# Stores of the projection stage on GpSimd's DMA queue, in one step of a hybrid retention and sliding-window layer

## The chip, the core and the metric

The kernel runs on one core of one Trainium2 chip. The metric is the device time of one execution in microseconds, the median of several runs. A core has TensorE (PE, matmuls), VectorE (DVE), ScalarE (ACT), GpSimd (POOL) and SyncE (SP). Each engine takes its instructions in order. DMA transfers are issued as instructions of an engine's queue, and all queues share the core's 16 DMA engines.

## The reference

One inference step of one layer over 1024 prompt tokens and 64 sample tokens, width 1024, in float32. The part that matters here is the mixer's input projection and the retention that follows it:

```python
rq, rk, rv, rg, sq, sk, sv, ga, gb = in_proj(h, g_attn, w_in)   # rms_norm(x) @ w_in, split
q = rope(rq.reshape(B, S, RET_HEADS, RET_DK), pos)
k = rope(rk.reshape(B, S, RET_HEADS, RET_DK), pos) * (RET_DK ** -0.5)
v = rv.reshape(B, S, RET_HEADS, RET_DV)
...
s = jnp.einsum('bihd,bjhd->bhij', q, k) * intra          # inside a chunk
o = jnp.einsum('bhij,bjhe->bihe', s, v)
o = o + jnp.einsum('bihd,bhde->bihe', q, state) * q_dec[None, :, :, None]
new_state = state * jnp.exp(log_gamma * C)[None, :, None, None] + kv
```

Four retention heads of 256, then a sliding-window attention (SWA) of 16 heads over `sq`, `sk`, `sv` with a relative-position bias, then gates, a mix, cross-attention and a SwiGLU feed-forward.

## The kernel before

All 1088 tokens are worked as two halves of 544 columns (`half(t)`), with the features on the 128 partitions. A projection (`strassen`, line 264) multiplies 1024 x 256 weights with the tokens in seven products of 24 matmuls, each operand split into a high and a low part. A product goes to one of three PSUM buffers (`bank_pair`); `taken` (line 594) adds it to a partial sum and writes it to one of eight stage tiles, which go round (`staged`, line 590).

The changed stage is `project_phase` (line 573). It runs, in program order:

- the values of head 0 (`values`, line 641), with plain products;
- for each head: keys and queries with rotation (`rotated`, line 618; four result tiles and four helper tiles each), the values (heads 1 to 3), one pair of SWA queries (`project` with `queries`, lines 602 and 647), then `retention(h)` (line 741);
- SWA's keys and values (line 687);
- the fourth pair of SWA queries, the gates and the memory's keys and values.

Everything that a projection makes is stored to scratch in DRAM and read back later: `d_qkv` (rotated keys, queries, values), `d_sq` (SWA queries, in rows of 64 numbers, 256 bytes), `d_skv`, `d_ret` (retention's output, line 875), and the states `o_rsp` and `o_rss` (lines 820, 848). `bias_table` (line 550) writes `d_rb`, 1 MB from 16 partitions. `retention` reads `d_qkv` back in blocks of 256 tokens into the buffers `ks`, `vf` and `qs`, one of each. Its first step on PE is to turn `ks` and `vf` (`turned`, L738); the scores (`pss`) come next.

For heads 0 and 1 VectorE does the whole rotation (L630 to L636); from head 2 on GpSimd does its last two steps (L635, L636). GpSimd also multiplies the SWA results by `rstd` (L605).

Both `load` (line 116) and `store` (line 119) issue on SyncE, so a store that waits for its data holds up every load behind it. The order of the instructions on each engine is not the program order: the framework lays it out when the program is built (`schedule_with_timeline_sim=True`), and `issue_after` pins a few places. In the retention of one head, the next head's projections are thus mixed in. [...]

```python
nc = bacc.Bacc("TRN2", target_bir_lowering=False, num_devices=1, dynamic_dma_scratch_size=1024)
```

Of the kernel before, what the change touches and what calls it, by code (L numbers as in the profile page):

```python
# [97 lines left out]
class Ring:  # L98


    def __init__(self, pool):
        self.pool, self.next = pool, 0
# [7 lines left out]
class Kernel:  # L110
    def __init__(self, nc, tc, io, decay):
        self.nc, self.tc, self.io, self.decay = nc, tc, io, decay
        self.later = []
        self.refill = None

    def load(self, out, in_):
        return self.nc.sync.dma_start(out, in_).ins

    def store(self, out, in_):
        self.nc.sync.dma_start(out, in_)  # L120

    def split(self, src, hi, lo):
        self.last_cast = self.nc.scalar.copy(hi, src).ins  # L123
# [449 lines left out]
    def project_phase(self):  # L573
        nc, tc, io = self.nc, self.tc, self.io
        with ExitStack() as ctx:
# [11 lines left out]
            half = lambda t: slice(t * HALF, (t + 1) * HALF)  # L587
            flat = lambda o: o.rearrange("p b c -> p (b c)")

            def staged():  # L590
                count[0] += 1
                return stage[(count[0] - 1) % len(stage)]

            def taken(ps, sb):
                o = staged()
                if sb is None:
                    nc.scalar.copy(o, ps)
                else:
                    nc.vector.tensor_tensor(out=o, in0=ps, in1=sb, op=ALU.add)  # L599
                return flat(o)  # L600

            def project(w, put, act=None, other=None):
                def emit(i, t, ps, sb):
                    o = taken(ps, sb)
                    (nc.vector if act is not None else nc.gpsimd).tensor_tensor(  # L605
                        out=o, in0=o, in1=self.rstd[:, half(t)], op=ALU.mult)
                    if act is not None:
                        nc.scalar.activation(o, o, act)
                    if other is not None:
                        r = op.tile([P, HALF], F32, tag="other", bufs=4, name="other")  # L610
                        self.load(r, other(i)[:, half(t)])
                        nc.gpsimd.tensor_tensor(out=o, in0=o, in1=r, op=ALU.mult)
                    put(i, t, o)
                cast = self.last_cast
                self.strassen(w, self.ops, emit)
                return cast

            def rotated(w, h, j):

                done = {}  # L620

                def emit(i, t, ps, sb):
                    done[i, t] = taken(ps, sb)
                    if (1 - i, t) not in done:
                        return
                    a, b = done[0, t], done[1, t]
                    cos, sin = (rope[:, i, half(t)] for i in range(2))
                    sa, sb = flat(staged()), flat(staged())
                    tt = nc.vector.tensor_tensor
                    tt(out=sa, in0=a, in1=sin, op=ALU.mult)  # L630
                    tt(out=sb, in0=b, in1=sin, op=ALU.mult)
                    tt(out=a, in0=a, in1=cos, op=ALU.mult)
                    tt(out=b, in0=b, in1=cos, op=ALU.mult)
                    tt = tt if h < 2 else nc.gpsimd.tensor_tensor
                    tt(out=a, in0=a, in1=sb, op=ALU.subtract)  # L635
                    tt(out=b, in0=b, in1=sa, op=ALU.add)  # L636
                    self.store(self.d_qkv[j, 2 * h, :, half(t)], a)
                    self.store(self.d_qkv[j, 2 * h + 1, :, half(t)], b)
                self.strassen(w, self.ops, emit)

            def values(w, h, by=self.strassen):
                def emit(i, t, ps, sb):
                    self.stores.append(self.load(self.d_qkv[2, 2 * h + i, :, half(t)], taken(ps, sb)))
                by(w, self.ops, emit)

            pair = lambda w, h: self.load_ops([io[w][2 * h + i] for i in range(2)])
            def queries(p):
                def put(i, t, o):
                    d = self.d_sq[p, :, :, i, :]
                    r = lambda x: x.rearrange("p (c q) -> p c q", q=64)  # L650
                    if t == 0:
                        self.store(d[:, 0:8, :], r(o[:, :512]))
                        self.store(d[:, 8, 0:32], o[:, 512:])
                    else:
                        self.store(d[:, 8, 32:64], o[:, :32])
                        self.store(d[:, 9:17, :], r(o[:, 32:]))
                return put

            self.stores = []
# [4 lines left out]
            stage, count = self.stage_tiles(), [0]  # L664
            with ExitStack() as rctx:
                self.ra = rctx.enter_context(tc.tile_pool(name="ra", bufs=1, reuse_waits="tile"))
                rope = self.ra.tile([P, 2, T], F32, name="rope")
                for t in range(2):
                    self.load(rope[:, :, half(t)], io["c_rope"][:, :, half(t)])
                for h in range(H):  # L670
                    rotated(pair("w_k", h) if h else first, h, 1)
                    if h == 0:
                        self.token_squares()
                    rotated(pair("w_q", h), h, 0)
                    if h == 0:
                        self.token_roots()
                        self.retention_setup()
                    else:
                        values(pair("w_v", h), h)
                    if h:  # L680
                        project(pair("w_sq", h - 1), queries(h - 1))
                    self.retention(h)
                    if h == 0:
                        self.spread_roots()
                    if h == 1:
                        self.later.append(self.bias_table)
                project(self.load_ops((io["w_sk"], io["w_sv"])), lambda i, t, o: self.store(self.d_skv[i, :, half(t)], o))
            self.sums_by = nc.gpsimd
            project(pair("w_sq", 3), queries(3))
            steps = [0, 0, 0, 0, 1, 2, 2, 3, 3, 3, 2, 0]  # L690
            for idx, w, act in ((1, "w_ga", AF.Sigmoid), (0, "w_rg", AF.Silu), (2, "w_gb", AF.Sigmoid)):
                for m in range(0, KT, 2):
                    if (idx, m) == (1, 6):
                        fctx.close()
                        self.sixth = self.left.enter_context(tc.tile_pool(name="sixth", bufs=1, reuse_waits="tile"))
                        self.last_held = self.turns
                        self.sums_pool(ctx)
                        op = ctx.enter_context(tc.tile_pool(name="op", bufs=1, reuse_waits="tile"))
                        mp = ctx.enter_context(tc.tile_pool(name="mp", bufs=1, reuse_waits="tile"))
                        self.dense_psum = lambda: self.norm_psum("pd")  # L700
                        memory = self.memory_phase(mp)
                    store = nc.gpsimd.dma_start if (idx, m) == (2, KT - 2) else nc.scalar.dma_start if idx else self.store
                    put = lambda i, t, o, idx=idx, m=m, store=store: store(self.d_gate[idx][m + i, :, half(t)], o)
                    other = None if idx else lambda i, m=m: self.d_ret[m + i]
                    with tc.issue_after(project(pair(w, m // 2), put, act, other)):
                        for i in range(steps.pop(0)):
                            if (idx, m, i) == (0, 6, 0):
                                with tc.issue_after(self.last_mm):
                                    next(memory)
                            else:  # L710
                                next(memory)
# [1125 lines left out]
```

## Time and profile before

| | |
|---|---|
| median of 3 runs | 2172.38 us (2171.64 to 2174.21) |
| the profiled execution | 2174.93 us, its span 2173.1 us |
| PE busy | 2139.7 us, 98% of the span |
| VectorE, ScalarE, GpSimd busy | 71%, 40%, 26% |
| granted clock, mean | 0.996 of full speed |
| SyncE's queue (q1) | 175058 packets, 278.18 MB |
| GpSimd's queue (q0) | 512 packets, 1.64 MB: eight DMAs, all after 780 us |
| the changed stage | from about 40 to 510 us of the span |

How to read it: a row of a timeline has the start in us, the length in us, the engine, the line, the operation, the tiles written and read, and in brackets the idle time before it and what ended that. SPq is SyncE's DMA queue; the length of an issue there is its time on the queue, not that of the transfer. A row of waits has who waited, for whom, the total in us, the number of times and the longest. A row of DMA issues ends with the count, the size of one and the median time from issue to landing.

### The profile page before, as it was taken

The page shows a single profiled execution, that of the slowest core. Times are in us where ns is not written, and L with a number is a line of the kernel's source. Part 1 is how long each engine was busy: PE and PEld are TensorE (multiplying, and loading weights), DVE is VectorE, ACT ScalarE, POOL GpSimd, SP SyncE. Part 2 cuts the span into 40 slices and gives each one's busy share as a digit, 9 for nine tenths or more (in the row PEclk, how much of TensorE's full clock was granted, in tenths as well). Part 3 has the DMA queues.
Part 4 walks back from the last instruction along what each step waited for, and adds up shares of the span by engine and source line. Part 5 has one row for each costly group of instructions (what it writes and reads, how often), then busy time and mean ns, then how long its engine had stood idle before and what let it go on. Part 6 is the DMA issues. An engine that isn't in the chain of part 4 may idle for free.

```text
span 2173.1 us, 41702 instructions
## 1 busy us (share of the span) xinstructions
PE 2139.7 (98%) x16371; PEld 2088.6 (96%) x16371; DVE 1546.5 (71%) x2870; ACT 876.2 (40%) x1900; POOL 562.2 (26%) x438
## 2 busy tenths in 40 slices
PE   9999999999999999999999999999999999999997
PEld 9999999999999997889999999999999999999997
DVE  8996978776677568656545465768777776777588
ACT  7444434244434347543233343333222222344243
POOL 0001211232253223430000000014565555523531
PEclk9999999999999999999999999999999999999999
DMA  6444453444345476327443111422343333384333
GB/s 225 146 140 118 128 139 110 138 130 153 118 144 171 161 223 224 117 87 228 123 152 103 40 54 54 153 81 91 126 132 106 105 103 114 100 327 144 120 113 114
DMA packets 180373, 290.83 MB, mean 134 GB/s; under 512 B 40178, under 2 KB 109202, under 8 KB 180178
## 3 DMA queue, kind: packets, MB, share of 16 engines
q1 hardware_dynamic: 175058, 278.18, 40.3%
q10 hardware_dynamic: 4608, 8.36, 1.0%
q8 instruction: 129, 2.11, 0.4%
q0 software_dynamic: 512, 1.64, 0.2%
q14 instruction: 66, 0.54, 0.1%
HBM read 196.95 MB, written 91.16 MB: 133 GB/s over the span
## 4 chain that ended last, share of the span: by engine, by line
PE 88%; DVE 5%; DMA 3%; ACT 2%; issue 2%; POOL 0%; SPq 0%; POOLq 0%; DVEq 0%; ACTq 0%
PE pq L225 18%; PE pq L223 18%; PE pq L222 18%; PE pd L156 8%; PE pd L158 7%; PE pd L157 7%; PE pout L1037 1%; PE pss L974 1%; DVE wq L124 1%; DMA hl<-d_op 1%; PE pk L738 1%; PE pp L1013 1%; DMA ld<-d_swa 1%; PE po L158 1%; PE po L157 1%
## 5 line engine op out<-in xcount | busy, mean ns | idle before, releaser
L124 DVE TENSOR_TENSOR wq<-raw,wq 128x512 fp32r<-128x512 f32 (+1 forms) x499 | 437.9, 882 | 134.8 <-ACT wq L123 131.7
L123 ACT CAST wq<-raw 128x512 fp32r<-128x512 f32 (+1 forms) x499 | 301.9, 614 | 539.0 <-PE pq L225 189.2
L223 PE MATMUL pq<-T,wq 128*128 128x272 f32 x1832 | 492.9, 289 | 0.0
L222 PE MATMUL pq<-T,wq 128*128 128x272 f32 x1832 | 491.3, 288 | 0.6 <-ACT wq L123 0.6
L223 PE MATMUL pq<-B,wq 128*128 128x272 f32 x1592 | 428.3, 289 | 2.1 <-DVE B L124 1.9
L222 PE MATMUL pq<-B,wq 128*128 128x272 f32 x1592 | 427.0, 288 | 0.5 <-ACT B L123 0.3
L225 PE MATMUL pq<-T,wq 128*128 128x272 f32 x1832 | 384.0, 290 | 0.9 <-DVE wq L124 0.9
L222 PEld LDWEIGHTS pq<-T,wq 128*128 128x128 f32 x1832 | 345.2, 188 | 1.2 <-issue 0.8
L223 PEld LDWEIGHTS pq<-T,wq 128*128 128x128 f32 x1832 | 344.9, 188 | 0.9 <-issue 0.8
L225 PE MATMUL pq<-B,wq 128*128 128x272 f32 x1592 | 332.2, 289 | 1.1 <-DVE wq L124 1.1
L223 PEld LDWEIGHTS pq<-B,wq 128*128 128x128 f32 x1592 | 299.8, 188 | 3.2 <-DVE B L124 2.7
L222 PEld LDWEIGHTS pq<-B,wq 128*128 128x128 f32 x1592 | 299.5, 188 | 1.0 <-ACT B L123 0.9
L225 PEld LDWEIGHTS pq<-T,wq 128*128 128x128 f32 x1832 | 290.7, 190 | 2.4 <-DVE wq L124 1.1
L200 POOL TENSOR_TENSOR raw<-raw 128x512 f32<-128x512 f32 (+1 forms) x44 | 64.1, 1457 | 832.3 <-DVE rs_r L311 485.6
L225 PEld LDWEIGHTS pq<-B,wq 128*128 128x128 f32 x1592 | 252.4, 190 | 2.5 <-DVE wq L124 1.3
L269 DVE TENSOR_TENSOR u<-pq,u 128x544 f32<-128x544 f32 x177 | 127.2, 719 | 80.9 <-PE pq L225 80.7
L605 POOL TENSOR_TENSOR stage<-stage,rstd 128x544 f32<-128x544 f32 x20 | 31.5, 1582 | 319.8 <-ACT rstd L500 205.6
L599 DVE TENSOR_TENSOR stage<-pq,u 128x544 f32<-128x544 f32 x112 | 80.5, 719 | 33.6 <-PE pq L225 29.1
L156 PE MATMUL pd<-xc,wq 128*128 128x256 f32 (+1 forms) x256 | 74.6, 291 | 0.0
L158 PE MATMUL pd<-xc,wq 128*128 128x256 f32 (+1 forms) x256 | 74.2, 290 | 0.0
L1485 POOL TENSOR_TENSOR stage<-stage,rstd_f 128x544 f32<-128x544 f32 x40 | 63.9, 1608 | 39.1 <-ACT stage L1484 39.1
L157 PE MATMUL pd<-xc,wq 128*128 128x256 f32 (+1 forms) x256 | 73.8, 288 | 0.0
(385 smaller groups left out, 4559.3 us busy)
## 6 DMA issues: line engine op xcount, KB each, us to landing
hl<-d_op SPq DMA_DIRECT2D x85, 272.0 KB, 5.0
d_qkv<-stage SPq DMA_DIRECT2D x44, 272.0 KB, 2.5
d_op<-stage SPq DMA_DIRECT2D x44, 272.0 KB, 2.3
d_op<-ht SPq DMA_DIRECT2D x44, 272.0 KB, 4.0
raw<-w_gate SPq DMA_DIRECT2D x22, 512.0 KB, 3.6
raw<-w_up SPq DMA_DIRECT2D x22, 512.0 KB, 4.9
raw<-w_down SPq DMA_DIRECT2D x16, 512.0 KB, 4.6
d_gate<-stage ACTq DMA_DIRECT2D x28, 272.0 KB, 2.8
```

Source lines behind the costliest of these rows:

```text
L123: self.last_cast = self.nc.scalar.copy(hi, src).ins
L124: return self.nc.vector.tensor_tensor(out=lo, in0=src, in1=hi.bitcast(F32), op=ALU.subtract).ins
L156: mm(ps, wh, xh, start=start, stop=False)
L157: mm(ps, wh, xl, start=False, stop=False)
L158: self.last_mm = mm(ps, wl, xh, start=False, stop=stop).ins
L200: tt(out=a11, in0=a11, in1=a21, op=sub)
L222: mm(ps[:, c, :HC], w[:, 0, ks], x[:, 0, cs], start=start, stop=False)
L223: mm(ps[:, c, :HC], w[:, 0, ks], x[:, 1, cs], start=False, stop=False)
L225: self.last_mm = mm(ps[:, c, :HC], w[:, 1, ks], x[:, 0, c * HC:(c + 1) * HC], start=False, stop=stop).ins
L269: add = lambda out, a, b: nc.vector.tensor_tensor(out=out, in0=a, in1=b, op=ALU.add)
L599: nc.vector.tensor_tensor(out=o, in0=ps, in1=sb, op=ALU.add)
L1485: nc.gpsimd.tensor_tensor(out=g, in0=g, in1=r[t], op=ALU.mult)
```

## The change

A new field `store_by` names the engine that issues stores. It is SyncE at first, GpSimd from the first rotated keys on until SWA's keys and values have been projected, and SyncE again from the fourth pair of SWA queries on. `values` now calls `store` where it called `load` (which also issues on SyncE) for its stores. In `queries`, the store of 8 blocks of 64 tokens becomes two of 4 blocks; the short stores of 32 tokens stay. Loads are untouched.

```diff
@@ -112,12 +112,13 @@
         self.nc, self.tc, self.io, self.decay = nc, tc, io, decay
         self.later = []
         self.refill = None
+        self.store_by = nc.sync
 
     def load(self, out, in_):
         return self.nc.sync.dma_start(out, in_).ins
 
     def store(self, out, in_):
-        self.nc.sync.dma_start(out, in_)
+        return self.store_by.dma_start(out, in_).ins
 
     def split(self, src, hi, lo):
         self.last_cast = self.nc.scalar.copy(hi, src).ins
@@ -640,7 +641,7 @@
 
             def values(w, h, by=self.strassen):
                 def emit(i, t, ps, sb):
-                    self.stores.append(self.load(self.d_qkv[2, 2 * h + i, :, half(t)], taken(ps, sb)))
+                    self.stores.append(self.store(self.d_qkv[2, 2 * h + i, :, half(t)], taken(ps, sb)))
                 by(w, self.ops, emit)
 
             pair = lambda w, h: self.load_ops([io[w][2 * h + i] for i in range(2)])
@@ -649,11 +650,13 @@
                     d = self.d_sq[p, :, :, i, :]
                     r = lambda x: x.rearrange("p (c q) -> p c q", q=64)
                     if t == 0:
-                        self.store(d[:, 0:8, :], r(o[:, :512]))
+                        for q in range(0, 8, 4):
+                            self.store(d[:, q:q + 4, :], r(o[:, q * 64:q * 64 + 256]))
                         self.store(d[:, 8, 0:32], o[:, 512:])
                     else:
                         self.store(d[:, 8, 32:64], o[:, :32])
-                        self.store(d[:, 9:17, :], r(o[:, 32:]))
+                        for q in range(0, 8, 4):
+                            self.store(d[:, 9 + q:13 + q, :], r(o[:, 32 + q * 64:288 + q * 64]))
                 return put
 
             self.stores = []
@@ -664,6 +667,7 @@
             stage, count = self.stage_tiles(), [0]
             with ExitStack() as rctx:
                 self.ra = rctx.enter_context(tc.tile_pool(name="ra", bufs=1, reuse_waits="tile"))
+                self.store_by = nc.gpsimd
                 rope = self.ra.tile([P, 2, T], F32, name="rope")
                 for t in range(2):
                     self.load(rope[:, :, half(t)], io["c_rope"][:, :, half(t)])
@@ -685,7 +689,7 @@
                     if h == 1:
                         self.later.append(self.bias_table)
                 project(self.load_ops((io["w_sk"], io["w_sv"])), lambda i, t, o: self.store(self.d_skv[i, :, half(t)], o))
-            self.sums_by = nc.gpsimd
+            self.sums_by, self.store_by = nc.gpsimd, nc.sync
             project(pair("w_sq", 3), queries(3))
             steps = [0, 0, 0, 0, 1, 2, 2, 3, 3, 3, 2, 0]
             for idx, w, act in ((1, "w_ga", AF.Sigmoid), (0, "w_rg", AF.Silu), (2, "w_gb", AF.Sigmoid)):
```

## The prediction

> **What bounds the kernel now.** I read the page first, then the waits of PE inside the stage that the change touches (40 to 510 us), then that stretch in windows, then the queues around the longest wait.
>
> ```profile
> PE 2139.7 (98%) x16371; PEld 2088.6 (96%) x16371; DVE 1546.5 (71%) x2870; ACT 876.2 (40%) x1900; POOL 562.2 (26%) x438
> PE 88%; DVE 5%; DMA 3%; ACT 2%; issue 2%; POOL 0%; SPq 0%; POOLq 0%; DVEq 0%; ACTq 0%
> ```
>
> PE bounds the kernel: it is busy 98% of the span and makes 88% of the chain that ended last; DMA makes 3%. A change of queues can only win what PE waits for a transfer. The waits of PE in the stage:
>
> ```profile
> PE pk L738 <- DMA ks<-d_qkv: 2.0, 1, 2.0
> PE pss L156 <- DVE rr L311: 1.5, 1, 1.5
> PE pq L225 <- DVE wq L124: 1.1, 1, 1.1
> ```
>
> Three waits, 4.6 us. Two of them end with VectorE, one with a transfer. Windows, with columns length, PE, PEld, DVE, ACT, POOL busy, granted clock, DMA share and GB/s:
>
> ```profile
> 226.00:236.00 10.00, 8.51 (x70) 8.32 (x69) 9.93 (x15) 4.27 (x12) 6.52 (x4) 1.00 0.31 105
> 316.00:320.00 4.00, 4.00 (x35) 4.00 (x34) 3.88 (x5) 1.72 (x4) 1.74 (x1) 1.00 0.92 101
> 331.00:334.00 3.00, 3.00 (x16) 3.00 (x15) 2.88 (x5) 3.00 (x10) 0.00 (x0) 0.53 0.21 37
> 334.00:337.00 3.00, 3.00 (x23) 3.00 (x23) 2.88 (x8) 0.82 (x4) 0.00 (x0) 0.90 0.34 138
> ```
>
> The 1.5 us wait lies in 226 to 236, where VectorE itself is full (9.93 of 10) and the clock stays at 1.00. Behind the 2.0 us wait the granted clock is 0.53 and then 0.90: 3 x 0.47 + 3 x 0.10 = 1.71 us of PE work lost on top. So the late load cost 1.95 + 1.71 = 3.66 us. Why it was late (rows of SyncE's and PE's timelines; the fifth is from the chain that ended last):
>
> ```profile
> 309.74 0.66 SPq L120 DMA_DIRECT2D d_rb<-rb  x1
> 312.82 9.30 SPq L120 DMA_DIRECT2D d_sq<-stage  x4
> 322.84 2.07 SPq L120 DMA_DIRECT2D d_sq<-stage  x2
> 325.00 0.39 SPq L117 DMA_DIRECT2D raw<-w_q  x1
> 325.49 4.44 DMA ks<-d_qkv
> 323.31 0.28 PE L158 MATMUL pss<-qs,ks 128*128 128x256 f32 x1
> 327.82 0.28 PE L225 MATMUL pq<-T,wq 128*128 128x272 f32 x1
> 330.06 0.30 PE L738 MATMUL pk<-ident,ks 128*128 128x128 f32 x1 [1.95 <-DMA ks<-d_qkv]
> ```
>
> The one `ks` buffer is free when the last score product that reads it ends, 323.31 + 0.28 = 323.59. SyncE then stands in query stores until 322.84 + 2.07 = 324.91 and issues a weight load before `ks` at 325.49: 1.90 us late. The load lands at 329.93 and PE, out of work since 328.10, starts at 330.06. 1.90 us earlier it lands at 328.03, just in time.
>
> **The change part by part.** *Stores off SyncE.* Of the stage's stores, 101 leave SyncE: 44 of rotated keys, queries and values, 20 of `d_ret`, 8 of states, 24 of `d_sq` (three pairs), 4 of `d_skv` and `d_rb`. The large query stores become two each, so GpSimd gets 113. The fourth pair stays on SyncE and issues 12 instead of 8. Four more issues of a third of a us delay nothing that PE waited for. The `ks` load no longer stands behind stores: **-3.66 us**. What is late next? VectorE and ScalarE stood idle around 330 for the same load (VectorE's 3.80 us are quoted below), so nothing else holds PE there. Bounds: -3.66, and 0 if the transfers themselves are the brake (a rival). I take -3.66, since 1.90 us of SyncE's delay covers the 1.95 us wait but for 0.05.
>
> *GpSimd's issue time.* The trace has eight DMAs on that queue; four are these:
>
> ```profile
> L703 POOL DMA_DIRECT2D d_gate<-stage x4 | 2.3, 585 | 22.6 <-ACT stage L608 22.6
> 60.00:475.00 415.00, 410.41 (x3262) 401.80 (x3262) 334.76 (x668) 168.52 (x377) 57.59 (x36) 1.00 0.43 128
> ```
>
> 113 x 0.585 = 66 us onto 57.59 of 415: 30% busy. If the 24 halves (512 rows, where the quoted store has 128) cost four times as much, 24 x 3 x 0.585 = 42 us more: 40%. Either way GpSimd doesn't bound the stage on average: 0. Queued behind its stores are its own multiplications (L605) and rotation sums (L635, L636), which release stage tiles and not PE directly.
>
> *Landing.* Same transfers from the two queues, median to landing:
>
> ```profile
> d_gate<-stage SPq DMA_DIRECT2D x16, 272.0 KB, 2.3
> d_gate<-stage POOLq DMA_DIRECT2D x4, 272.0 KB, 3.6
> d_mv<-mo SPq DMA_DIRECT2D x6, 128.0 KB, 1.7
> d_mv<-swin POOLq DMA_DIRECT2D x2, 128.0 KB, 3.8
> ```
>
> A store lands 1.3 to 2.1 us later. Only head 0 has loads that follow their stores closely (later heads have the value and query projections between):
>
> ```profile
> 95.49 0.32 SPq L120 DMA_DIRECT2D d_qkv<-stage  x1
> 98.66 0.37 SPq L117 DMA_DIRECT2D qs<-d_qkv  x1
> 103.26 0.62 ACT L123 CAST qs<-qs 128x512 fp32r<-128x512 f32 x1 [4.28 <-DMA qs<-d_qkv]
> 104.47 0.28 PE L156 MATMUL pss<-qs,ks 128*128 128x256 f32 x1
> ```
>
> The cast ends at 103.88 and PE uses it at 104.47: 0.59 us of cover. PE loses 1.3 - 0.59 = 0.7 to 2.1 - 0.59 = 1.5 us. The nearest row is the one of equal size: **+0.7 us**. [...]
>
> *The stage tiles.* Eight tiles go round. The query projection of pair 0 fills four, which GpSimd multiplies in one burst once `rstd` is there; the keys of head 2 need them again soon after:
>
> ```profile
> 206.05 5.75 POOL L605 TENSOR_TENSOR stage<-stage,rstd 128x544 f32<-128x544 f32 x4 [205.60 <-ACT rstd L500]
> 213.03 2.08 SPq L120 DMA_DIRECT2D d_sq<-stage  x4
> 218.67 0.72 DVE L630 TENSOR_TENSOR stage<-stage,rope 128x544 f32<-128x544 f32 x1
> 326.60 0.73 DVE L630 TENSOR_TENSOR stage<-stage,rope 128x544 f32<-128x544 f32 x1
> 331.12 0.69 DVE L124 TENSOR_TENSOR st<-state,st 128x512 fp32r<-128x512 f32 x1 [3.80 <-ACT st L123]
> ```
>
> L630 at 218.67 writes the seventh tile, the third query tile. Before, all stores were issued by 215.11. Whether large halves overlap on GpSimd's queue no row shows. Low end: they overlap, 0.585 us each, and the tile is free long before: 0. High end: one at a time, 3.8 us each (the 128 KB row of this queue). From 207.5 the sixth half is issued at 207.5 + 5 x 3.8 = 226.5 and lands at 230.3, 11.6 us after VectorE wants the tile, with everything behind L630 in VectorE's queue waiting too. Between: the rotation is put behind other work of VectorE; then four of its instructions, 4 x 0.72 = 2.9 us, move into 226 to 236, where VectorE is full and PE already waits for it. The build orders each engine's queue anew, and it can see a tile that comes free late, so I take the middle: **+2.9 us**. At the next such place (326.60, pair 1) the same deferral costs 0, for VectorE is idle 3.80 us there.
>
> **Sum:** -3.66 + 0.7 + 2.9 = -0.1 us. The profiled execution took 2174.93 us (span 2173.1 and 1.8 around it), 2.55 above the median 2172.38. Against its own time the sum gives 2174.8; moved to the median, **2172.3 us**: no change.
>
> **Rivals.** *Everything hidden* (chance 0.25). The halves overlap, `qs` is covered: -3.66, 2168.7. With a new order the two waits on VectorE could go too (1.5 + 1.1): -6.3, 2166.1. For it: 1.90 us of queueing is all that the `ks` load lacked. Against it: VectorE is full exactly where these waits lie.
>
> *Large stores one at a time, slower* (0.35). A half on GpSimd's queue isn't issued until the half before it has landed, and VectorE stops at a stage tile. Places: 218.67 (11.6 us late, above) and 326.60. There `d_rb` goes first:
>
> ```profile
> d_rb<-rb SPq DMA_DIRECT2D x1, 1024.0 KB, 12.7
> 700.00:780.00 80.00, 80.00 (x660) 80.00 (x659) 48.85 (x70) 34.67 (x59) 16.50 (x12) 1.00 0.51 169
> ```
>
> From its landing at 322.4 the fourth half behind it is issued 3 x 3.8 later and lands at 337.6: 11.0 us late. PE has some cover: while VectorE stands, two more products fit the PSUM buffers, each 24 matmuls at 80.00 / 660 = 0.121 us, 5.8 us in all. The first place then costs 11.6 - 5.8 + 1.71 for the clock = 7.5, the second 11.0 - 5.8 + 1.71 = 6.9 in place of today's 3.66. With the 0.7 that is +11.4: 2183.8; without the cover 11.6 more, 2195. It decides from a period per half of 2.8 us (207.5 + 6 x 2.8 = 218.67 + 5.8, rounded). For it: the halves exist at all, and line 1815 gives the build a DMA scratch of only 1024 bytes. Against it: the new order may move the rotations away from the late tiles. [...]
>
> *The transfers are the brake* (0.07): the change frees the queue but not the load. For it: DMA engines 92% busy at 101 GB/s from 316 to 320, which `d_rb` and the query stores fill wherever they were issued. Against it: the buffer was free at 323.59, when `d_rb` had landed. Then the 3.66 stays: +0.7, 2173.1, with the 2.9 up to 2176.0.
>
> **How the numbers follow.** Two times of this kernel can be told apart from about 0.2%, 4.3 us: faster is below 2168.0, slower above 2176.7. Forecast 0.33, its own range 2169 to 2176 (ends: nothing lost at the tiles, twice the 2.9 or 1.5 for `qs`); everything hidden 0.25, of which 0.17 below 2168.0; one at a time 0.35, all slower; brake 0.07. Faster 0.17 and 0.01 of the forecast's case: 0.18. Slower 0.35 and 0.02 each of the forecast's and the brake's cases: 0.39. Same: 0.43. The range runs from the hidden case's 2166.1, 1 us lower for what a new order does elsewhere, 2165, to 2188, which holds the slower case but for the part with little cover: about 0.1 is left out above, under 0.1 below.
>
> **What would show it.** No wait of PE on `ks` near 325, and the clock at 1.00 there: the first step. GpSimd's DMA rows at some 0.6 us, stage multiplications starting right behind each other: overlap. Gaps of about 3.8 us between the halves, or long DMA rows on GpSimd, and VectorE waiting for `d_sq`: one at a time, and whether PE then waits for VectorE tells its price. PE waiting for `qs` near 104 by up to 1.5 us: the landing term. The forecast is wrong if the waits of PE between 40 and 510 us sum to under 2 us or to more than 10, or if the time moved outside that stretch.

## The result and the profile after

The changed kernel takes 2193.54 us (median of 6 runs, 2189.06 to 2195.22); the kernel before, run beside it, 2173.57 us (2171.64 to 2177.18). The ratio is 1.0087 with a 95% interval of 1.0076 to 1.0098: slower by about 19 us, more than the forecast's range and more than the slower rival's 2183.8. The profiled execution took 2192.82 us, its span 2191.0 against 2173.1.

Busy times of the changed kernel, and the waits of PE between 40 and 530 us (total, times, longest):

```profile
PE 2143.6 (98%) x16371; PEld 2090.3 (95%) x16371; DVE 1553.0 (71%) x2870; ACT 877.2 (40%) x1900; POOL 629.9 (29%) x551
...
PE pss L157 <- DVE rr L312: 7.3, 1, 7.3
PE pb L876 <- DVE sf L795: 5.4, 1, 5.4
PE pss L157 <- DVE kt L774: 1.7, 2, 1.4
PE pq L226 <- DVE wq L125: 1.1, 1, 1.1
PE pb L876 <- DVE vb L783: 0.4, 1, 0.4
```

(Line numbers are one higher than before from L115 on, and four higher behind L667.) No wait names `ks` any more, and none `qs`: what the change was to remove is removed. In its place PE waits 7.3, 5.4 and 1.7 us for VectorE, 1.4 of the 1.7 just ahead of the 5.4. VectorE's own waits for the query stores in the same stretch, and two rows of its timeline:

```profile
DVE stage L631 <- DMA d_sq<-stage: 10.2, 2, 8.9
DVE stage L600 <- DMA d_sq<-stage: 3.4, 1, 3.4
...
334.10 0.68 DVE L125 TENSOR_TENSOR st<-state,st 128x512 fp32r<-128x512 f32 x1
343.63 0.72 DVE L631 TENSOR_TENSOR stage<-stage,rope 128x544 f32<-128x544 f32 x1 [8.85 <-DMA d_sq<-stage]
```

VectorE stands from 334.78 to 343.63 at a rotation that writes a stage tile, because the tile's store has not landed. GpSimd's timeline shows why the store is late (start, duration, and in brackets the idle time before the row):

```profile
206.04 6.21 POOL L606 TENSOR_TENSOR stage<-stage,rstd 128x544 f32<-128x544 f32 x4 [3.23 <-ACT rstd L501]
212.19 0.79 POOL L121 DMA_DIRECT2D d_sq<-stage  x1
215.00 1.30 POOL L121 DMA_DIRECT2D d_sq<-stage  x2 [2.02 <-issue]
217.75 0.76 POOL L121 DMA_DIRECT2D d_sq<-stage  x1 [1.45 <-issue]
...
227.84 1.30 POOL L121 DMA_DIRECT2D d_sq<-stage  x2 [2.01 <-issue]
230.57 0.75 POOL L121 DMA_DIRECT2D d_sq<-stage  x1 [1.43 <-issue]
233.27 0.76 POOL L121 DMA_DIRECT2D d_sq<-stage  x1 [1.95 <-issue]
...
d_sq<-stage POOLq DMA_DIRECT2D x24, 128.0 KB, 2.4
```

An issue takes 0.76 us, but the next half comes about 2.7 us after the one before (230.57 to 233.27), a little more than the 2.4 us to landing; a small store (128 rows) can go with a half, hence the x2. Between them GpSimd stands ("issue": it waits for nothing that the profile shows), and it goes on when the half in flight has landed: by the trace the half issued at 230.57 lands at 232.94, and the next is issued at 233.27. Halves that take longer to land hold the next one longer: 3.4 us to landing for the one of 217.75, the next half at 221.51; 7.8 us for the one of 321.26, the next at 329.24. What a stop costs PE is seen in windows (length, PE, PEld, DVE, ACT, POOL busy, granted clock, DMA share, GB/s):

```profile
240.00:245.00 5.00, 2.13 (x10) 2.17 (x11) 4.50 (x9) 2.82 (x6) 3.09 (x4) 0.64 0.30 111
245.00:250.00 5.00, 5.00 (x32) 5.00 (x30) 3.06 (x6) 0.62 (x1) 0.72 (x1) 0.68 0.48 161
345.00:350.00 5.00, 0.00 (x0) 0.00 (x0) 3.88 (x9) 1.45 (x4) 1.30 (x2) 0.72 0.66 213
350.00:355.00 5.00, 4.08 (x22) 4.11 (x23) 5.00 (x16) 1.05 (x3) 0.00 (x0) 0.59 0.05 6
```

The granted clock is low in these windows (it is 1.00 from 250 and from 355 on), which adds about 5.00 x 0.32 + 2.13 x 0.36 = 2.4 us at the first place and 4.08 x 0.41 = 1.7 us at the second.

To see where all of the 17.9 us of span lie, two landmarks in PE's order are followed through the runs (starts of the first and the last of a group): the memory phase's sum over `macc`, behind the changed stage, and the last SWA output `pout`. Rows of before and after:

```profile
L326 PE MATMUL pt<-ones,macc x4: 164/251/252, 652.0 to 652.3; 128*128 128x2 f32 x4
L1037 PE MATMUL pout<-pT,swin x256: 375/379/431, 820.9 to 973.5; 64*64 64x256 f32 x64, 128*64 128x256 f32 x64
```

```profile
L327 PE MATMUL pt<-ones,macc x4: 165/251/251, 666.0 to 666.3; 128*128 128x2 f32 x4
L1041 PE MATMUL pout<-pT,swin x256: 376/379/431, 832.9 to 992.1; 64*64 64x256 f32 x64, 128*64 128x256 f32 x64
```

The first landmark comes 14.0 us later, the stretch from it to the second grows from 321.5 to 326.1 (+4.6), the rest goes from 1199.6 to 1198.9 (-0.7). So there are two losses: 14.0 us in the stage with the moved stores, and 4.6 us in SWA, where the change edits nothing. Of the 14.0, 13.7 are found in PE's waits and clock: 15.9 + 2.4 + 1.7 = 20.0 us in the changed kernel, 4.6 + 1.71 = 6.3 before. The 4.6 shows mostly as one wait (800 to 1050 us of the changed kernel):

```profile
PE pd L157 <- ACT swin L957: 4.6, 1, 4.6
```

The same reading for every run of this study (ratios to the kernel before, which was run beside each; the three columns from the profiled executions):

| run | ratio, 95% interval | to `macc` | to last `pout` | to the end |
|---|---|---|---|---|
| before | 1 | 652.0 | 321.5 | 1199.6 |
| changed | 1.0087 (1.0076 to 1.0098) | 666.0 | 326.1 | 1198.9 |
| e1 changed, 1536 bytes | 1.0024 (1.0011 to 1.0037) | 648.9 | 325.9 | 1201.9 |
| e2 quarters | 1.0038 (1.0024 to 1.0052) | 653.6 | 324.5 | 1197.7 |
| e3 queries back on SyncE | 1.0048 (1.0033 to 1.0063) | 657.5 | 324.4 | 1200.0 |
| e4 queries alone | 1.0038 (1.0025 to 1.0051) | 658.9 | 320.9 | 1200.8 |
| e5 queries alone, 1536 bytes | 0.9987 (0.9977 to 0.9998) | 648.6 | 319.6 | 1202.5 |
| e6 1536 bytes, rotated back | 1.0008 (0.9998 to 1.0018) | 651.1 | 321.4 | 1198.1 |
| e7 `d_rb` alone | 0.9999 (0.9990 to 1.0008) | 651.9 | 319.9 | 1199.6 |
| e8 halves on SyncE | 1.0010 (0.9999 to 1.0021) | 650.8 | 320.7 | 1199.6 |
| e9 `d_rb` back on SyncE | 1.0068 (1.0046 to 1.0090) | 660.7 | 326.9 | 1197.8 |
| e10 pair 0 alone | 1.0009 (0.9997 to 1.0021) | 654.2 | 319.7 | 1198.3 |
| e11 pair 1 alone | 1.0006 (0.9995 to 1.0017) | 654.7 | 321.1 | 1197.7 |
| e12 queries on ScalarE | 0.9985 (0.9976 to 0.9994) | 649.4 | 320.5 | 1198.9 |

The columns come from one profile each. In e7 and e8, which leave the orders of PE, VectorE and ScalarE as they were, they differ from the kernel before by up to 1.2 and 1.6 us, and the last column spreads over 4.8 us, so a difference of a us or two in them says little.

### The profile page after: what moved, and what is told of

The parts are those of the page before. It is cut to its first block, busy times and chain, and to the rows that moved or that the text cites. A ratio compares the mean times of both kernels' runs of the same rounds, so it can differ in the third digit from the quotient of the medians.

```text
span 2191.0 us, 41751 instructions
## 1 busy us (share of the span) xinstructions
PE 2143.6 (98%) x16371; PEld 2090.3 (95%) x16371; DVE 1553.0 (71%) x2870; ACT 877.2 (40%) x1900; POOL 629.9 (29%) x551
## 5 line engine op out<-in xcount | busy, mean ns | idle before, releaser
L125 DVE TENSOR_TENSOR wq<-raw,wq 128x512 fp32r<-128x512 f32 (+1 forms) x499 | 445.5, 897 | 137.3 <-ACT wq L124 134.0
L121 POOL DMA_DIRECT2D d_qkv<-stage x44 | 24.4, 555 | 179.6 <-DVE stage L637 120.7
```

Source lines behind the costliest of these rows:

```text
L125: return self.nc.vector.tensor_tensor(out=lo, in0=src, in1=hi.bitcast(F32), op=ALU.subtract).ins
```

## The experiments

The theories: A, only one half at a time fits into the DMA scratch of line 1815 (the "space" of the expectations), so the halves go one at a time; B, GpSimd itself takes 2.7 us for a half, whatever the scratch; C, the build's new order of the engines loses the time; E, the other moved stores do. The runs show what the size of the scratch does to the halves; what it holds, none of them shows.

**e1: more DMA scratch.**

```diff
-dynamic_dma_scratch_size=1024
+dynamic_dma_scratch_size=1536
-out = lambda: mp.tile([P, NMEM], F32, tag="mo", bufs=4, name="mo")
+out = lambda: mp.tile([P, NMEM], F32, tag="mo", bufs=3, name="mo")
```

> The changed kernel, with a DMA scratch of 1536 bytes in place of 1024 (and three tiles of the memory phase's output in place of four, which makes the room). Theory A (the halves of the query stores are issued one at a time because only one fits into the space for GpSimd's descriptors, and that stops VectorE at a stage tile, then PE): two halves now fit, their DMA rows come in twos, mean period near 1.4 us in place of 2.7, VectorE's waits for d_sq at L631 fall from 10.2 us to under 3, the median to 2170 to 2180. Theory B (GpSimd itself needs 2.7 us to make the descriptors of a half, whatever the space): period 2.7 us as before, median 2189 to 2196. Theory C (the loss comes from the build's new order of the engines, not from the stores): waits of PE and median about as in the changed kernel, though the period changes.

Every engine's order of instructions is that of the changed kernel, row for row, so only the space (and one tile of the memory phase, behind the stage) differs. GpSimd's rows, the waits of VectorE for the query stores, and the waits of PE between 40 and 530 us:

```profile
212.37 2.09 POOL L121 DMA_DIRECT2D d_sq<-stage  x3
215.19 0.76 POOL L121 DMA_DIRECT2D d_sq<-stage  x1 [0.73 <-issue]
216.47 1.29 POOL L121 DMA_DIRECT2D d_sq<-stage  x2 [0.52 <-issue]
...
222.47 1.50 POOL L121 DMA_DIRECT2D d_sq<-stage  x2 [0.57 <-issue]
...
DVE stage L631 <- DMA d_sq<-stage: 2.7, 1, 2.7
DVE stage L600 <- DMA d_sq<-stage: 0.3, 1, 0.3
...
PE pq L226 <- DVE wq L125: 1.1, 1, 1.1
PE pss L157 <- DVE rr L312: 1.1, 1, 1.1
PE pb L876 <- DVE sf L795: 0.3, 1, 0.3
```

The eight halves of pair 0 leave within 212.37 to 223.97, 1.45 us each, and PE's waits fall to 2.5 us. The ratio goes from 1.0087 to 1.0024: 0.63%, 13.7 us, was the space. B falls, and C falls for the stage: with the same order the loss there is gone. To `macc` this run is 3.1 us faster than the kernel before. C stays for the 4.4 us in SWA.

**e2: smaller stores.** Parts of 256 rows in place of 512 (`range(0, 8, 2)` for `range(0, 8, 4)`, both halves).

> The changed kernel, with each large query store in four parts of 256 rows in place of two of 512, still on GpSimd's queue, scratch 1024 bytes. Theory A: three parts fit at once, so a half's worth takes between 1.45 us (two issues of 0.72) and 1.8 us (2.7 x 2 / 3) in place of 2.7; VectorE's waits for d_sq fall below half of 10.2 us, median 2172 to 2182. Theory B (time per row): 2.7 us for two parts, median 2188 to 2196. Theory D (one DMA at a time on this queue, whatever its size): 2 x 2.4 = 4.8 us per half, median above 2200.

Ratio 1.0038, VectorE waits for no query store at all, and where nothing holds them the parts go out at 0.73 us, three of them in 2.20 us before a gap of 0.22:

```profile
211.62 2.20 POOL L121 DMA_DIRECT2D d_sq<-stage  x3
214.04 2.01 POOL L121 DMA_DIRECT2D d_sq<-stage  x3 [0.22 <-issue]
```

Several small parts fit where one half did: A again; B and D (one DMA at a time of whatever size) fall. The time is not all won back: up to `macc` this run is still 1.6 us slower than the kernel before, its order is another than e1's, and PE waits 0.8 us for `ks`. Why is open.

**e3: the query stores back on SyncE**, whole, all else as changed.

```diff
-                        for q in range(0, 8, 4):
-                            self.store(d[:, q:q + 4, :], r(o[:, q * 64:q * 64 + 256]))
-                        self.store(d[:, 8, 0:32], o[:, 512:])
+                        nc.sync.dma_start(d[:, 0:8, :], r(o[:, :512]))
+                        nc.sync.dma_start(d[:, 8, 0:32], o[:, 512:])
```

> The changed kernel, with the query stores of all four pairs whole and on SyncE's queue as in the kernel before; all other moved stores stay on GpSimd's. Theory A: no wait for d_sq on VectorE, the loss is gone, median 2168 to 2175; below 2172 only if the ks load no longer stands behind query stores. Theory E (the later landing of the 44 stores of d_qkv and the others on GpSimd's queue costs the time): median 2185 to 2194, with waits of PE on loads of d_qkv. Theory C (new order): above 2180 with PE's waits on VectorE where no DMA is late.

1.0048, about 2182: a miss for A, and under E's 2185 to 2194. The time fits C's range (above 2180), but not its sign, since the longest wait of PE is on a late load. E's waits on `d_qkv` loads came in another way. SyncE's rows:

```profile
317.89 4.62 SPq L657 DMA_DIRECT2D d_sq<-stage  x1
322.62 4.23 SPq L118 DMA_DIRECT2D vf<-d_qkv  x1
...
329.69 0.38 SPq L118 DMA_DIRECT2D ks<-d_qkv  x1
```

With `d_rb` issued by GpSimd at 314.89, SyncE still stands 4 to 5 us in the issue of a query store and of a load behind it; PE then waits 3.6 us for `ks`, and its granted clock from 300 to 350 is 0.93 in place of 0.97: by an estimate from these 46.41 x 0.07 = 3.2 us more, 6.8 in all, where the same estimate for the kernel before gives 1.95 + 48.05 x 0.03 = 3.4. `d_rb` took 12.7 us to landing in the kernel before and 12.3 in the changed one, which puts its landing here, by an estimate, at about 327: two of SyncE's issues took 4.62 and 4.23 us before that, though SyncE didn't issue `d_rb` itself. e7 tests `d_rb` alone.

**e4: the query stores alone**, in halves, pairs 0 to 2 on GpSimd; the rest as before.

```diff
+                    by = nc.gpsimd.dma_start if p < 3 else nc.sync.dma_start
-                        self.store(d[:, 0:8, :], r(o[:, :512]))
-                        self.store(d[:, 8, 0:32], o[:, 512:])
+                        for q in range(0, 8, 4):
+                            by(d[:, q:q + 4, :], r(o[:, q * 64:q * 64 + 256]))
+                        by(d[:, 8, 0:32], o[:, 512:])
```

> The kernel before, with only the query stores of pairs 0 to 2 moved to GpSimd's queue in halves (pair 3 in halves on SyncE). Theory A: this part alone carries the loss, period of the halves 2.7 us, VectorE waiting for d_sq some 8 to 14 us, median 2184 to 2196. Theory E: 2168 to 2175, no loss. Theory C leaves it open, 2170 to 2195.

2181.20 us, 1.0038, under A's 2184, and VectorE waits 4.2 us for `d_sq`, under the 8 to 14 expected: this part alone loses 6.9 us to `macc`, half of the 14.0, and nothing in SWA (320.9).

**e5: the same with 1536 bytes** (and the `mo` tiles as in e1).

> The kernel of the run before it (the kernel before, only the query stores of pairs 0 to 2 on GpSimd's queue in halves), with 1536 bytes of DMA scratch and three output tiles of the memory phase; every engine's order is the same as there. Theory A (space for one half's descriptors): the first part, up to the memory phase's PE sum, takes about 3 us less than in the kernel before (652.0) in place of 6.9 us more; SWA as there; median 2167 to 2171, under the kernel before. Theory B: 2179 to 2183 as there.

Every engine's order is that of e4. To `macc` 648.6, 10.3 us less than e4; no wait on `ks` or `d_sq`; 2169.91 us beside 2171.89. A holds, and the version beats both kernels, by little: 0.9987, interval 0.9977 to 0.9998.

**e6: changed, 1536 bytes, the rotated keys and queries back on SyncE** (L638 and L639 with `nc.sync.dma_start`). The build then writes SyncE's queue in SWA as in the kernel before: there a store of `d_mix` comes after one `d_gate` load, in the changed kernel only after a second one, which stands for its buffer, and after the load of `swin` from `d_sq`:

```profile
821.72 0.37 SPq L117 DMA_DIRECT2D swin<-d_gate  x1
822.18 0.38 SPq L120 DMA_DIRECT2D d_mix<-swin  x1
823.51 0.32 SPq L117 DMA_DIRECT2D swin<-d_gate  x1
824.03 0.37 SPq L117 DMA_DIRECT2D swin<-d_sq  x1
```

```profile
811.06 5.59 SPq L118 DMA_DIRECT2D swin<-d_gate  x2
816.83 0.85 SPq L118 DMA_DIRECT2D swin<-d_sq  x1
817.77 0.46 SPq L121 DMA_DIRECT2D d_mix<-swin  x1
```

(First e4, with the order of before, then e1, with that of the changed kernel.)

> The changed kernel with 1536 bytes, and the 32 stores of rotated keys and queries back on SyncE's queue; all other moved stores stay on GpSimd's. The build then writes SyncE's loads and stores in SWA in the order of the kernel before. Theory C' (the 4 to 5 us still lost with 1536 bytes lie in SWA and come from that order alone): no wait of PE for swin above 1 us in SWA, the stretch from the memory phase's PE sum to the last SWA output takes 320 to 323 us as in the kernel before (321.5), median 2167 to 2172. Theory E (the stores that GpSimd still carries cost those us): the stretch takes 324 to 326 as with all stores moved, median 2173 to 2177.

From `macc` to the last `pout` 321.4, as before: C' for SWA. The wait at L957 falls from 4.7 to 0.2, though one of 1.9 at L1173 stands beside it, more than the 1 expected. The median, 2173.59, lies 1.6 above C's range and inside E's, since only 0.9 us is gained up to `macc`. The other runs bear this out: the five with +3 to +5 in this stretch (changed, e1, e2, e3, e9) all have this store in the later place and a wait of 3.6 to 4.8 us at the same line (L957, in e3 L955), and none of the other nine kernels has the store there or such a wait. GpSimd has two neighbouring steps of SWA the other way round in the same five, and no run changes one of the two alone.

**e7: `d_rb` alone on GpSimd.**

> The kernel before, with only the d_rb store (1 MB) on GpSimd's queue. Theory H (SyncE's queue was held by standing behind that store): the ks load is issued when its buffer is free, no wait of PE on ks, median 2167 to 2170. Theory I (the DMA engines are full of that store wherever it is issued, and SyncE's query stores stall behind it as in the run with the query stores on SyncE): SyncE's rows of d_sq still take 2 us and more, the ks load stays late, median 2171 to 2176.

0.9999, and SyncE's row of the query stores is as long as before, 9.70 us against 9.30; PE still waits 2.0 us for `ks`:

```profile
312.65 9.70 SPq L120 DMA_DIRECT2D d_sq<-stage  x4
```

I holds: moving the large store alone gains nothing, so the query stores are what to move.

**e8: the halves on SyncE**, as a control for the split.

> The kernel before, with the large query stores in halves but all on SyncE's queue. Theory A: the split itself costs nothing, as SyncE issues a part in about 0.4 us; no wait for d_sq on VectorE above 2 us, median 2170 to 2175. Theory G (the split costs the time, by more DMAs in flight or more issues): above 2178.

1.0010 (0.9999 to 1.0021): the split costs nothing that this measurement can tell.

**e9: changed (1024 bytes), `d_rb` back on SyncE.**

> The changed kernel (1024 bytes) with only the d_rb store back on SyncE's queue; VectorE's, PE's and ScalarE's orders are those of the changed kernel. Theory K (d_rb sits in the space for descriptors until it lands, and so holds up the query stores of pair 1 behind it on GpSimd's queue by some 7 us): the gap of 7.4 us before a query store near 329 shrinks to under 3, PE's wait of 7.3 us near 351 falls below 3 and its clock there stays near 1, median 2182 to 2188; the wait of 5.4 us near 243 (pair 0) stays. Theory K' (the halves' own period is what counts at pair 1 too): PE's wait near 351 stays above 5, median 2190 to 2195.

2188.52 us, 1.0068, half a us above K's range and under that of K'. PE's 7.3 us wait for `rr` becomes 2.6 with the clock at 1.00 behind it, the one of 5.4 us at pair 0 stays, and the first landmark comes 5.3 us earlier. So `d_rb` on the same queue made pair 1 dearer. But the gap that K wanted under 3 us is 6.29, although `d_rb` is on another queue. In the changed kernel the half that was issued at 321.26, while `d_rb` (316.56, 12.3 us to landing) was in flight, took 7.8 us to landing, where the median is 2.4; that the half of the first row was held up in the same way is an estimate from that:

```profile
322.61 1.34 POOL L121 DMA_DIRECT2D d_sq<-stage  x2 [0.31 <-POOL stage L606]
330.24 0.76 POOL L121 DMA_DIRECT2D d_sq<-stage  x1 [6.29 <-issue]
```

K is right on the wait and wrong on its reason in part; how much comes from `d_rb`'s place on that queue and how much from its traffic stays open.

**e10 and e11: one pair's halves on GpSimd** (e4 with `p == 0`, then `p == 1`).

> The kernel before, with the query stores in halves and only those of pair 0 on GpSimd's queue (1024 bytes). Theory A with the places priced apart: pair 0 carries most of the loss of the run with pairs 0 to 2, PE loses 5 to 8 us between 200 and 250 (waits and clock), the ks wait near 330 stays at 2 to 3, median 2177 to 2181. If pair 1 carries it: 2171 to 2175.

> The kernel before, with the query stores in halves and only those of pair 1 on GpSimd's queue (1024 bytes), d_rb on SyncE's. Theory A with the places priced apart: no wait on ks near 330 as SyncE is free of those stores (-3.7), a wait on VectorE of 2 to 5 us in its place, median 2169 to 2175. By the rival as it stands in the prediction (6.9 in place of 3.66): 2174 to 2177.

2176.81 and 2174.80 us, 1.0009 and 1.0006, both within what can be told from no change; the first lies just under A's range, the second in A's and in the rival's. To `macc` they lose 2.2 and 2.7 us, together 4.9 of e4's 6.9. In e10 the `ks` wait fell to 0.6 without being touched, as the order around it moved, which hid part of pair 0's price (a wait of 4.9 us for VectorE). In e11 no wait on `ks` is left, but one of 4.7 us on VectorE is. Which pair carries more is not settled by them; the rival's 6.9 in place of 3.66, +3.2, is near e11's 2.7.

**e12: the query stores of pairs 0 to 2, whole, on ScalarE's queue**, all else as before.

```diff
+                    by = nc.scalar.dma_start if p < 3 else nc.sync.dma_start
-                        self.store(d[:, 0:8, :], r(o[:, :512]))
-                        self.store(d[:, 8, 0:32], o[:, 512:])
+                        by(d[:, 0:8, :], r(o[:, :512]))
+                        by(d[:, 8, 0:32], o[:, 512:])
```

> The kernel before, with the query stores of pairs 0 to 2 whole on ScalarE's queue. Theory L (any queue that isn't held by GpSimd's space gains the ks load): no wait on ks, no wait for d_sq above 3 us, median 2167 to 2171. Theory M (behind d_rb the issuing engine itself stands for up to 9 us, as SyncE did, and on ScalarE that holds its casts): ScalarE's DMA rows of 2 us and more near 315 to 325, PE waiting for ScalarE, median 2174 to 2185.

2170.23 us, 0.9985 (0.9976 to 0.9994), in L's range: the other version that beats both kernels, with no change of memory. ScalarE does stand at one issue, as M had it, but behind it lies slack (the 5.72 us without a cast are its own issues):

```profile
313.57 3.86 ACTq L657 DMA_DIRECT2D d_sq<-stage  x1
317.47 0.76 ACTq L656 DMA_DIRECT2D d_sq<-stage  x1
319.32 0.62 ACT L123 CAST wq<-raw 128x512 fp32r<-128x512 f32 x1 [5.72 <-DMA d_sq<-stage]
```

PE's one wait for ScalarE in the stage is 0.7 us, and none is on `ks`.

## Why the prediction was wrong

Both signs that it had named for being wrong came: PE's waits in the stage sum to 15.9 us, more than 10, and 4.6 us were lost outside it.

**Stores off SyncE, -3.66: right.** The `ks` wait is gone, or 0.8 us (e2), wherever the query stores of pairs 0 to 2 all left SyncE. With the second loss taken out, the gain can be read: to `macc` 3.1 us in e1, 3.4 in e5, 2.6 in e12. Moving the query stores alone gains it (e5, e12), moving `d_rb` alone doesn't (e7).

**GpSimd's issue time, 0: right.** POOL's busy time rose from 562.2 to 629.9 for 113 more issues, about 0.60 us each, inside the 66 to 108 us of the prediction, and in e1 that load costs PE nothing in the stage.

**Landing, +0.7: too much, its size wrong.** The term took the 1.3 us between two groups of `d_gate` stores. The moved stores themselves, before and after:

```profile
d_qkv<-stage SPq DMA_DIRECT2D x44, 272.0 KB, 2.5
```

```profile
d_qkv<-stage POOLq DMA_DIRECT2D x44, 272.0 KB, 2.8
```

0.3 us later, under the 0.59 us of cover, and no wait on `qs`. With the term at 0 the sum is 2171.6: four stores among other traffic, which gave the 1.3, were a poor price for this queue.

**The stage tiles, +2.9: this is the step that failed.** The prediction chose a middle between halves that overlap and halves that go singly, on the ground that the build would defer four rotations into 226 to 236, where VectorE is full and PE waits for it. The build moved them little: in e1, which has the order of the changed kernel, the four rotations at this place start from 227.93 to 232.31, in the kernel before from 225.16 to 232.67. In that window of e1 VectorE's rows follow one another without a gap, and PE is busy 49.69 of the 50 us from 200 to 250, at clock 1.00 (48.51 before), and waits only 0.3 us near there (the `sf` row; its 1.1 for `rr` lies behind 300). So a full VectorE cost PE nothing there. The order helps nothing either: it is the same for both sizes of the space, and in the changed kernel VectorE stopped at whatever stood next in its queue, which is what puts the same four at 231.14 to 238.85. The term had two states in these runs, not a middle: near 0 (e1), or the rival's loss.

**The rival one at a time is what happened; it was put too low.** e1 and e5, beside the changed kernel and e4, are two pairs of runs in which only the scratch changes the stage: with 1536 bytes in place of 1024 the halves of pair 0 leave 1.45 us apart in e1, 2.7 in the changed kernel, and the stage is 17.1 and 10.3 us shorter (to `macc`, 666.0 to 648.9 and 658.9 to 648.6). The rival's period of 3.8 us was too long (2.7 measured), and by its own threshold of 2.8 the first place would then cost nothing; but it let the first half leave at 207.5, after the first product, while GpSimd's queue puts all four products first and the first half leaves at 212.19. Five periods 1.1 us too long and a start 4.7 us too early nearly cancel, by luck: its sixth half was to land at 230.3, and the tile that VectorE waits for is free at 230.38.

What made it too low is the cover: the rival subtracted PE's cover from VectorE's lateness and stopped there. At the first place VectorE stands 3.41 us and then 1.34, less than the 5.8 of cover, yet PE loses 1.4 + 5.4 us of waits and 2.4 of clock, 9.2 where the rival had 7.5. VectorE reaches `sf`, which PE waits for, at 241.99, in e1 with the same order at 235.51: of these 6.48 us 4.75 are the two stops, and the rest is mostly small operations (L313 took 3.21 us in place of e1's 0.15, L310 0.16 in place of 1.32), on which the last section has more. At the second place VectorE stands 8.85 us (11.0 reckoned), and PE did have cover, 8.8 us, from VectorE's stop at 334.78 to PE's at 350.92 - 7.32 = 343.60, more than the 5.8 reckoned; still 7.3 + 1.7 = 9.0 us were lost where the rival had 6.9. VectorE starts again at 343.63, but what PE waits for stands far behind that rotation in its queue:

```profile
350.69 0.15 DVE L312 RECIPROCAL rr<-rr 128x2 f32<-128x2 f32 x1
```

The wait of 7.3 us is VectorE's backlog, worked off from 343.63 to 350.84 when the cover was already spent (for 1.12 us of it VectorE waits for a load of weights). The cover must hold the stop and the work that piles up in it.

**Outside the stage:** the range allowed 1 us for a new order elsewhere; SWA took 4.6. Nothing in the profile of before prices that; e6 shows that an order of SyncE's and GpSimd's rows that comes and goes with 32 stores some 300 us earlier is worth it.

**The transfers are the brake** fell as put, for `ks` is no longer waited for; a milder form would fit e3 and e9, where, beside the store of 1 MB, two of SyncE's issues took 4.62 and 4.23 us and a half left after a gap of 6.29.

## What to carry to other kernels

Before stores go to GpSimd's queue, measure how close together they leave it. Here, with 1024 bytes of scratch, halves of 128 KB went one per landing time (2.7 us apart, 2.4 us to landing), with 1536 bytes one per 1.45 us. Then ask which tiles these stores release, and what stands behind the first instruction that wants one. The price of such a stop is lateness plus the backlog behind it, less the cover, and on top what the clock loses (2.4 and 1.7 us here, nothing behind the stop of 2.6 us in e9). Here the gain needed one queue change only, the query stores to ScalarE (e12), and the rest of the change bought nothing (to `macc`, e1 gains 3.1 us with all the stores moved and e5 3.4 with the query stores alone).

## What was not expected of the hardware

An engine that issues on its own queue stood after 1 MB had been issued on another: 4.62 and 4.23 us on SyncE from 317.89 (e3, `d_rb` issued at 314.89), 3.86 on ScalarE from 313.57 (e12, `d_rb` at 306.57), rows that on SyncE mostly take 0.3 to 0.6 us. By the 12.3 to 12.7 us that `d_rb` took to landing in the changed kernel and before, it was still in flight then: an estimate. No run leaves that transfer out, so it is not shown to be the cause.

A VectorE operation on 128x2 elements took 3.21 us in the changed kernel, where the same line took 0.16 before:

```profile
233.54 3.21 DVE L313 TENSOR_TENSOR rs_t<-rr 128x2 f32<-128x2 f32 x1
```

```profile
234.04 1.37 POOL L637 TENSOR_TENSOR stage<-stage 128x544 f32<-128x544 f32 x1
235.37 1.36 POOL L636 TENSOR_TENSOR stage<-stage,stage 128x544 f32<-128x544 f32 x1
```

It ends at 236.75, GpSimd's second sum at 236.73. Two more rows of 128x2 in the changed kernel end so: L315 (239.49, 1.28 us) at 240.77, beside a sum that ends at 240.76, and L319 (241.09, 0.97 us) at 242.06, beside one that ends at 242.05. In e1, with the same order on every engine, GpSimd's sums fall at other times and the slow rows go with them: L313 starts at 231.49, beside no sum, and takes 0.15 us, while L315 (232.95, 1.31 us) ends at 234.26, beside a sum that ends at 234.24. Why they end together no run shows. In the changed kernel the sums came late because the stores ahead of them in GpSimd's queue did, and fell on small operations that stand ahead of `sf`.
